# Hybrid S5, attention and mixture-of-experts block: gelu in two halves, each behind its own S5 outputs

## The chip, the cores and the metric

One core of a Trainium2 chip runs the whole block in one launch. The metric is the device time of an execution in microseconds, lower is better; a kernel's time is the median of several executions. TensorE (PE) does the matmuls, VectorE (DVE), ScalarE (ACT) and GpSimd (POOL) the elementwise work, and the queue of SyncE (SP) issues nearly all loads.

## The reference

The input is 256 tokens of 1024 channels. What the block computes, shortened:

```python
h = rms_norm(x, ln1_g)
u, q, k, v, gates = split(h @ w_in)                 # 512, 512, 512, 512, 2048 columns
y_ssm = s5_mixer(u, ...)                            # 32 groups, 64 complex states: a scan over the tokens
g = gelu(y_ssm)                                     # tanh form, 512 channels
y_ssm = g * sigmoid(g @ w_glu + b_glu)
y_attn = moba_attention(q, k, v, rel_bias)          # 8 heads; 256 tokens are one block, so causal softmax
merged = sigmoid(gate_ssm) * (y_ssm @ w_up_ssm) + sigmoid(gate_attn) * (y_attn @ w_up_attn)
x = x + merged @ w_out
x = x + hier_moe(rms_norm(x, ln2_g), ...)           # 32 experts, w1, w3: 1024 x 512, w2: 512 x 1024, two per token
return rms_norm(x, ln_f_g)
```

## The kernel before

The **front** is everything up to the router: the input projection as sixteen column slices (units `in0` to `in15`, 256 columns each, run in the order 0 to 8, 12, 9, 13, 10, 14, 11, 15), the GLU matmul (unit `glu`, which runs between `in11` and `in15`), the up projections (`up0` to `up3`) and the output projection (`out0` to `out3`). Units from `in12` on, `glu`, `up` and `out` run in split precision: a weight slice is loaded (`raw`, two buffers, blocks 2 and 3), cast to a high part `wh`, the difference goes to a low part `wl` (`split`, lines 711 and 714, two buffers of each), and three products are summed on PE. While a unit's matmuls run, the next unit's slice is split and the one two units on is loaded (`next_raw`).

The **back** is the mixture of experts: 8 quads of 4 experts, every quad 24 pieces of 1 MB of weights (16 of w1 and w3, 8 of w2), so 192 pieces in all. `pump` issues one piece each on the SP queue into the next of 22 slots (`KN['slots']`); a slot is one of the kernel's blocks of 1 MB, and most blocks hold something else in the front. A piece whose block is still in use waits at the head of the SP queue. `KN['after']` says how many pieces are issued behind the load of which unit: 15 in the front, the other 7 of the first 22 behind `out3`.

**Background threads** (`pool_thread`, `ssm_thread`, `attn_thread`, `gelu_thread`) are generators. `bg()` runs one step of those that are due after each quarter of an input slice's matmuls; the table `KN['g']` gives how many ticks a step waits, `KN['e']` which engine does an elementwise operation (V is DVE, A is ACT, G is POOL; E is "expand directly on the engine that multiplies"). So the tables set the order in which instructions stand in each engine's queue, and each engine runs its queue in that order. What is left of the threads when `glu` is reached is emitted in one go (`while threads: bg()`), ahead of the GLU matmuls.

The S5 part works on four channel groups j of 128 channels, in two halves hb (groups 0 and 1, then 2 and 3): prepare `W1e` and `Pe`, transpose into `M1s`, matmul `stp` (`s5_S`), scan on DVE, matmul `yp` (`s5_y`), then `s5_out` (lines 1149 and 1151) writes the outputs `yT`. Block 10 (`Uy`) holds the S5 inputs `U` and the outputs `yT`. Attention runs in two halves of four heads; its result `ya` sits in block 15, the block that the second half's scan coefficients `E` held. `gelu_thread` waits for the whole of S5 and of attention, and writes `gel` to block 8 and its split `gHL` to block 11; per group it is ACT square (`q`), DVE (`a`), ACT tanh (`t`), DVE (`b`), then the split (`s`).

Of the kernel before, what the change touches and what calls it, by code (L numbers as in the profile page):

```python
# [50 lines left out]
for _n, _w in (("ident", 128), ("tri", 128), ("iota1", 32), ("iota0", 32), ("rev", 32)):  # L51
# [391 lines left out]
       'geluge0a': 0,  # L443
       'geluge0b': 30,
       'geluge0q': 1,
       'geluge0s': 22,
       'geluge0t': 0,
       'geluge1a': 0,
# [1 line left out]
       'geluge1q': 1,  # L450
       'geluge1s': 6,
       'geluge1t': 26,
       'geluge2a': 26,
       'geluge2b': 13,
       'geluge2q': 1,
       'geluge2s': 16,
       'geluge2t': 1,
       'geluge3a': 40,
       'geluge3b': 5,
       'geluge3q': 1,  # L460
       'geluge3s': 22,
       'geluge3t': 13,
# [118 lines left out]
    'pump': {'glu0.0': 1,  # L581
       'glu0.1': 0,
       'in10.0': 0,
       'in10.1': 1,
       'in11.0': 0,
       'in11.1': 1,
       'in12.0': 0,
       'in12.1': 0,
       'in13.0': 0,
       'in13.1': 0,  # L590
       'in14.0': 0,
       'in14.1': 1,
       'in15.0': 1,
       'in15.1': 0,
       'in7.1': 0,
       'in8.1': 0,
       'in9.0': 0,
       'in9.1': 0,
       'out0.0': 0,
       'out0.1': 2,  # L600
       'out1.0': 0,
       'out1.1': 0,
       'out2.0': 0,
       'out2.1': 20,
       'up0.0': 2,
       'up0.1': 0,
       'up1.0': 1,
       'up1.1': 0,
       'up2.0': 0,
       'up2.1': 0,  # L610
       'up3.0': 1,
       'up3.1': 0},
    'slots': [16, 18, 20, 19, 21, 10, 11, 22, 8, 15, 17, 14, 13, 9, 12, 3, 2, 4, 0, 1, 6],
# [35 lines left out]
KN['pump'] = {}
KN['after'] = {'in9': 1, 'in11': 2, 'glu': 2, 'in15': 1, 'up1': 2, 'up3': 2, 'out0': 1, 'out1': 2, 'out2': 1}  # L650
KN['nw'] = 1
KN['warm'] = 10
KN['SL'] = 1
KN['after'] = {'in9': 1, 'in11': 2, 'glu': 2, 'in15': 1, 'up1': 2, 'up3': 2, 'out0': 1, 'out1': 2, 'out2': 1}
KN['slots'] = [20, 16, 18, 17, 21, 19, 10, 11, 8, 22, 13, 15, 12, 14, 9, 3, 7, 2, 4, 0, 1, 6]
# [1454 lines left out]
```

## Time and profile before

| | us |
|---|---|
| three runs | 662.68, 664.0, 664.91 |
| median | 664.0 |
| the profiled execution, its own time | 664.66 |
| its span, from the first to the last instruction | 662.9 |

The profiled execution is 0.66 us above the median. All rows further down are of it, and their clock starts at the span's first instruction. A mean clock of TensorE of 0.859 stands for a mix of its two levels, 1.2 and 2.4 GHz (0.50 and 1.00).

### The profile page before, as it was taken

How to read it: one execution, taken by the hardware profiler on the slowest of the kernel's cores; microseconds unless marked ns; L12 is line 12 of the kernel's file. 1: busy time of each engine (PE TensorE's matmuls, PEld its weight loads, DVE VectorE, ACT ScalarE, POOL GpSimd, SP SyncE). 2: the span in 40 equal slices, each digit the busy share in tenths (PEclk: the TensorE clock that was granted, in tenths of full speed). 3: DMA queues.
4: the chain of work that ended last, by engine and by line, in shares of the span. 5: the costliest groups of instructions: out<-in, count | busy, mean ns of one | idle time of the engine just before them, and what ended most of it. 6: DMA issues, size and time to landing. Idle time of an engine off the chain costs nothing.

```text
span 662.9 us, 9490 instructions
## 1 busy us (share of the span) xinstructions
PE 526.3 (79%) x3903; PEld 287.1 (43%) x3903; DVE 204.6 (31%) x403; ACT 122.8 (19%) x280; POOL 137.6 (21%) x235
## 2 busy tenths in 40 slices
PE   8989999979999789886786667767767767686772
PEld 7768799969987435340042014102300410140121
DVE  5854998867684331110020011001101000111012
ACT  3461644665213010000010000001000000000111
POOL 4896855735453000000000000000000000000012
PEclk9999998998999699897669679766976886787877
DMA  8527353976897899999999999999999999999992
GB/s 304 190 75 242 130 223 128 360 276 224 304 375 294 337 421 426 426 426 426 427 427 426 428 427 426 426 428 426 427 427 426 428 427 426 427 426 425 428 405 85
DMA packets 35152, 235.00 MB, mean 355 GB/s; under 512 B 4051, under 2 KB 5244, under 8 KB 7452
## 3 DMA queue, kind: packets, MB, share of 16 engines
q1 hardware_dynamic: 34412, 231.98, 85.6%
q0 software_dynamic: 256, 1.74, 1.0%
q8 instruction: 32, 0.52, 0.3%
q10 hardware_dynamic: 432, 0.59, 0.3%
q14 instruction: 20, 0.16, 0.1%
HBM read 233.23 MB, written 2.63 MB: 356 GB/s over the span
## 4 chain that ended last, share of the span: by engine, by line
DMA 63%; PE 14%; DVE 8%; POOL 8%; ACT 3%; issue 3%; SPq 0%; ACTq 0%; POOLq 0%; DVEq 0%
DMA wslot<-in_w 56%; PE inp L1304 3%; PE pa L1899 2%; PE pb L1899 2%; DVE wl L714 1%; PE xgp L1880 1%; DMA rbz<-rbd 1%; PE py L1956 1%; PE glp L1478 1%; DMA raw<-in_w_up 1%; DMA raw<-in_w_out 1%; DMA xc<-in_x_ch 1%; DMA rbd<-t 1%; DMA raw<-in_w_in 1%; DVE mt L714 1%
## 5 line engine op out<-in xcount | busy, mean ns | idle before, releaser
L1899 PE MATMUL pb<-wslot,xg 128*32 128x512 f32 x512 | 91.5, 797 | 37.0 <-DMA wslot<-in_w 36.9
L1899 PE MATMUL pa<-wslot,xg 128*32 128x512 f32 x512 | 89.7, 782 | 34.4 <-DMA wslot<-in_w 34.4
L1956 PE MATMUL py<-wslot,mt 128*32 128x256 f32 x1024 | 73.0, 431 | 20.3 <-DMA wslot<-in_w 14.8
L1858 POOL DMA_DIRECT2D lnf<-in_ln_f x1 | 0.6, 607 | 386.2 <-DMA wslot<-in_w 386.2
L1942 DVE SCALAR_TENSOR_TENSOR mt<-mt,pa 128x512 f32<-128x512 f32 x8 | 5.5, 688 | 240.0 <-ACT mt L1941 240.0
L1899 PEld LDWEIGHTS pb<-wslot,xg 128*32 128x32 f32 x512 | 13.4, 123 | 109.7 <-DMA wslot<-in_w 95.2
L1956 PEld LDWEIGHTS py<-wslot,mt 128*32 128x32 f32 x1024 | 32.3, 121 | 61.2 <-DMA wslot<-in_w 27.1
L1899 PEld LDWEIGHTS pa<-wslot,xg 128*32 128x32 f32 x512 | 12.2, 121 | 99.2 <-DMA wslot<-in_w 86.5
L714 POOL TENSOR_TENSOR wl<-raw,wh 128x512 fp32r<-128x512 f32 (+1 forms) x22 | 39.4, 1795 | 29.8 <-ACT wh L711 22.3
L1882 DVE TENSOR_TENSOR xg<-xgp,sm 128x512 f32<-128x512 f32 (+2 forms) x19 | 11.5, 608 | 80.8 <-PE xgp L1880 80.8
L1971 PE MATMUL xacc<-mt 128*128 128x512 f32 x56 | 30.2, 666 | 5.3 <-ACT mt L1968 5.3
L1880 PEld LDWEIGHTS xgp<-mt,x 128*128 128x128 f32 x256 | 30.9, 200 | 6.9 <-issue 6.1
L1880 PE MATMUL xgp<-mt,x 128*128 128x128 f32 x256 | 32.8, 287 | 1.1 <-DVE mt L1873 1.1
L1941 ACT ACTIVATE mt<-pa 128x512 f32<-128x512 f32 x8 | 4.8, 597 | 155.1 <-PE pa L1899 155.1
L1968 ACT COPY mt<-py 128x512 f32<-128x512 f32 (+1 forms) x17 | 9.5, 561 | 120.9 <-PE py L1956 120.9
L714 DVE TENSOR_TENSOR wl<-raw,wh 128x512 fp32r<-128x512 f32 (+1 forms) x26 | 28.7, 1112 | 9.9 <-ACT wh L711 7.7
L1300 PE MATMUL inp<-hn,raw 128*128 128x256 f32 x128 | 28.7, 380 | 1.1 <-DVE vu L1319 1.1
L1304 PE MATMUL inp<-hH,wh 128*128 128x256 f32 x112 | 29.2, 296 | 0.0
L1304 PE MATMUL inp<-hL,wh 128*128 128x256 f32 x112 | 28.5, 289 | 0.0
L1300 PEld LDWEIGHTS inp<-hn,raw 128*128 128x128 f32 x128 | 23.9, 190 | 4.9 <-DVE vu L1319 1.8
L711 ACT CAST wh<-raw 128x512 fp32r<-128x512 f32 (+1 forms) x28 | 20.6, 768 | 20.2 <-POOL wl L714 9.2
L1304 PEld LDWEIGHTS inp<-hH,wh 128*128 128x128 f32 x112 | 22.2, 198 | 0.3 <-issue 0.2
(322 smaller groups left out, 734.9 us busy)
## 6 DMA issues: line engine op xcount, KB each, us to landing
wslot<-in_w SPq DMA_DIRECT2D x191, 1024.0 KB, 19.6
raw<-in_w_in SPq DMA_DIRECT2D x14, 1024.0 KB, 5.1
raw<-in_w_up SPq DMA_DIRECT2D x4, 1024.0 KB, 7.2
raw<-in_w_out SPq DMA_DIRECT2D x4, 1024.0 KB, 6.8
rbz<-rbd POOLq DMA_DIRECT2D x1, 1536.0 KB, 8.4
xc<-in_x_ch SPq DMA_DIRECT2D x4, 256.0 KB, 5.1
raw<-in_w_in SPq DMA_DIRECT2D x4, 256.0 KB, 5.9
raw<-in_w_in SPq DMA_DIRECT2D x2, 512.0 KB, 7.4
```

Source lines behind the costliest of these rows:

```text
L711: (A.copy if e is A else e.tensor_copy)(out_, in_)
L714: pick_engine(name, default, opts).tensor_tensor(out=out, in0=in0, in1=in1, op=op)
L1300: T.matmul(ps[:, 0:S], raws["in", u][:, k, c], (h32 if u < 3 else hn)[:, k], start=(k == 0), stop=(k == KD - 1))
L1304: T.matmul(ps[:, 0:S], (wh if x else wl)[:, k, c], (hH if y else hL)[:, k], start=first, stop=last)
L1478: T.matmul(ps[:, 0:S], (glh if x else gll)[:, k, c], (gH if y else gL)[:, k], start=first, stop=last)
L1880: T.matmul(ps[:, i * 128:i * 128 + 128], h2[:, b, k * 128:k * 128 + 128], Dts[:, b].rearrange("p e s -> p (e s)"), start=(b == 0), stop=(b ...
L1882: V.tensor_tensor(out=xg[:, ks[0]:ks[0] + n], in0=ps[:, 0:n * 128].rearrange("p (k n) -> p k n", k=n), in1=smc("g2", ks[0], ks[0] + n).uns ...
L1899: T.matmul(pab[t][32 * e:32 * e + 32], xg[:, k, 32 * e:32 * e + 32], w[:, e], start=(k == 0), stop=(k == KD - 1))
L1942: V.scalar_tensor_tensor(out=hid, in0=hid, scalar=1.0, in1=pab[0], op0=OP.add, op1=OP.mult)
L1956: T.matmul(py[32 * e:32 * e + 32, n % 2 * 256:n % 2 * 256 + 256], hidT[:, f, 32 * e:32 * e + 32], w[:, i, e], start=(f == 0), stop=(f == 3))
L1968: A.copy(ye[:, o % 512:o % 512 + m], py[:, o % 512:o % 512 + m])
L1971: T.matmul(xacc[2 * b + o // 512], DwT[:, b], ye, start=(qd == 0), stop=(qd == NQ_RUN - 2))
```

## The change

`gelu_thread` no longer waits for all of S5 and all of attention: it runs on groups 0 and 1 as soon as their outputs are written, and on groups 2 and 3 behind theirs. Its result overwrites the S5 inputs `U` of the same groups, which have no reader left by then. The split `gHL` goes to block 8, once the last scores of attention have read q and k there. The attention result `ya` goes to block 20 (the first half's `E`), no longer to block 15. Steps of the two groups alternate: q, q, a, a, t, t, b, b, split, split. The tables of engines, ticks and flush positions are new throughout; about 30 elementwise operations change engine. The slots and the places of the 15 early pieces are laid out anew: the piece behind `in9` and one of the two behind `glu` move to `up0` and `up2`.

```diff
-       'W3.0': 'V',
+       'W3.0': 'G',
...
-       'glu.1l': 'V',
+       'glu.1l': 'G',
...
-       'P1.1.1': 'V',
+       'P1.1.1': 'G',
...
-KN['slots'] = [20, 16, 18, 17, 21, 19, 9, 10, 11, 8, 22, 13, 15, 12, 14, 3, 7, 2, 4, 0, 1, 6]
-KN['after'] = {'in9': 1, 'in11': 2, 'glu': 2, 'in15': 1, 'up0': 1, 'up1': 2, 'up3': 2, 'out0': 1, 'out1': 2, 'out2': 1}
+    'slots': [16, 18, 17, 15, 21, 19, 11, 8, 10, 22, 9, 13, 20, 12, 14, 3, 7, 2, 4, 0, 1, 6],
+    'after': {'glu': 1, 'in11': 2, 'in15': 1, 'out0': 1, 'out1': 2, 'out2': 1, 'up0': 2, 'up1': 2, 'up2': 1, 'up3': 2},
...
             s5_out(j1, y1)
+            st["done"].add(("yo", j1))
             yield "yo%d" % j1
...
-                yield from until("scan", 1)
+                yield from until("scan", 0)
...
-                    yaH, yaL = carve(blk(15, "ya", F32R), (4, S), (4, S))
+                    yaH, yaL = carve(blk(20, "ya", F32R), (4, S), (4, S))
...
     def gelu_thread():
-        yield from until("ssm")
-        yield from until("attn")
-        gel, ge1 = carve(blk(8, "gel"), (4, S), (4, S))
-        if "glu" in native:
-            gH = gL = None
-        else:
-            gH, gL = carve(blk(11, "gHL", F32R), (4, S), (4, S))
-        st["g"] = gel, gH, gL
-
-        for j in range(4):
-            n = "ge%d" % j
-            A.activation(out=ge1[:, j], in_=yT[:, j], func=AF.Square, scale=math.sqrt(0.044715))
-            yield n + "q"
-            V.scalar_tensor_tensor(out=ge1[:, j], in0=ge1[:, j], scalar=1.0, in1=yT[:, j], op0=OP.add, op1=OP.mult)
-            yield n + "a"
-            A.activation(out=ge1[:, j], in_=ge1[:, j], func=AF.Tanh, scale=math.sqrt(2.0 / math.pi))
-            yield n + "t"
-        for j in range(4):
-            n = "ge%d" % j
-            V.scalar_tensor_tensor(out=gel[:, j], in0=ge1[:, j], scalar=1.0, in1=yT[:, j], op0=OP.add, op1=OP.mult)
-            yield n + "b"
-            if "glu" not in native:
-                split(n + "s", gel[:, j], gH[:, j], gL[:, j])
-                yield n + "s"
+        gel = [U[:, 4 * j:4 * j + 4].rearrange("p q c -> p (q c)") for j in range(4)]
+        st["g"] = [gel, None, None]
+
+        for js in ((0, 1), (2, 3)):
+            yield from until("yo", js[-1])
+            for f, n in enumerate("qatb"):
+                for j in js:
+                    if f == 0:
+                        A.activation(out=gel[j], in_=yT[:, j], func=AF.Square, scale=math.sqrt(0.044715))
+                    elif f == 2:
+                        A.activation(out=gel[j], in_=gel[j], func=AF.Tanh, scale=math.sqrt(2.0 / math.pi))
+                    else:
+                        V.scalar_tensor_tensor(out=gel[j], in0=gel[j], scalar=1.0, in1=yT[:, j], op0=OP.add, op1=OP.mult)
+                    yield "ge%d%s" % (j, n)
+            if "glu" in native:
+                continue
+            if js[0] == 0:
+                yield from until("scores")
+                st["g"][1:] = carve(blk(8, "gHL", F32R), (4, S), (4, S))
+            for j in js:
+                split("ge%ds" % j, gel[j], st["g"][1][:, j], st["g"][2][:, j])
+                yield "ge%ds" % j
```

Line numbers of the changed kernel are 31 to 34 lower than those of before in this part: 1445 and 1451 (DVE) become 1413, 1443 is 1409, 1447 is 1411, 1388 is 1357, 711 and 714 are 677 and 680.

**DVE, from the last softmax of attention to the end of gelu**, before (`yp` are the S5 outputs in PSUM, `pv` the attention outputs, `wl<-raw,wh` the split of the GLU weights):

```order
L1385 TENSOR_SCALAR fs<-fs 128x4
L1149 STREAM_TRANSPOSE Uy<-yp 128x2x4x32
L1151 SCALAR_TENSOR_TENSOR Uy<-vu,sm,Uy 128x256
L1149 STREAM_TRANSPOSE Uy<-yp 128x2x4x32
L1151 SCALAR_TENSOR_TENSOR Uy<-vu,sm,Uy 128x256
L714 TENSOR_TENSOR wl<-raw,wh 128x4x256 x2
L714 TENSOR_TENSOR ya<-pv,ya 128x256 x2
L1445 SCALAR_TENSOR_TENSOR gel<-gel,Uy 128x256 x4
L1451 SCALAR_TENSOR_TENSOR gel<-gel,Uy 128x256
L711 CAST gHL<-gel 128x256
L1451 SCALAR_TENSOR_TENSOR gel<-gel,Uy 128x256 x3
L714 TENSOR_TENSOR gHL<-gel,gHL 128x256
```

The same place in the changed kernel:

```order
L1354 TENSOR_SCALAR fs<-fs 128x4
L680 TENSOR_TENSOR wl<-raw,wh 128x4x256
L1115 STREAM_TRANSPOSE Uy<-yp 128x2x4x32
L1117 SCALAR_TENSOR_TENSOR Uy<-vu,sm,Uy 128x256
L1115 STREAM_TRANSPOSE Uy<-yp 128x2x4x32
L1117 SCALAR_TENSOR_TENSOR Uy<-vu,sm,Uy 128x256
L1413 SCALAR_TENSOR_TENSOR Uy<-Uy 128x256 x4
L680 TENSOR_TENSOR gHL<-Uy,gHL 128x256
L680 TENSOR_TENSOR ya<-pv,ya 128x256 x2
```

Gelu of groups 2 and 3 now stands ahead of the attention result, one split of the GLU weights ahead of the S5 outputs, the other on POOL; groups 0 and 1 are gone from here.

**ACT, from the cast of `in9` (before) to the casts of `in9` and `in13`** (`M1s<-m1p` copies the transposes that `stp` needs, `Pe` and `s5a` are S5 coefficients), before:

```order
L711 CAST wh<-raw 128x8x128
L1044 COPY Pe<-s5a 64x8x16
L1045 ACTIVATE Pe<-s5a 64x8x16
L1332 ACTIVATE thg<-inp,fs 128x256
L1044 COPY Pe<-s5a 64x8x16
L1045 ACTIVATE Pe<-s5a 64x8x16
L711 COPY attB<-ptp 128x512
L711 COPY Pe<-pprep 64x4x4x16 x2
L1332 ACTIVATE thg<-inp,fs 128x256
L711 COPY Pe<-pprep 64x4x4x16 x2
L711 COPY M1s<-m1p 128x512
L711 CAST wh<-raw 128x8x128 x2
```

The same place in the changed kernel, to the first cast, which is that of the second half of `in9`:

```order
L1357 ACTIVATE attB<-attB,fs 128x128 x4
L1409 ACTIVATE Uy<-Uy 128x256 x2
L1010 COPY Pe<-s5a 64x8x16
L1011 ACTIVATE Pe<-s5a 64x8x16
L677 COPY Pe<-pprep 64x4x4x16 x2
L1411 ACTIVATE Uy<-Uy 128x256
L1299 ACTIVATE thg<-inp,fs 128x256
L1411 ACTIVATE Uy<-Uy 128x256
L677 COPY attB<-ptp 128x512
L1299 ACTIVATE thg<-inp,fs 128x256
L677 CAST wh<-raw 128x8x128
L677 COPY M1s<-m1p 128x512
```

(The pair of lines 1010 and 1011 stands there twice.) Squares and tanh of groups 0 and 1 have come in, and four scalings of the softmax that DVE did; the cast of the first half of `in9` (now on DVE) and two `Pe` copies have gone, and the copy to `M1s` stands behind the first cast.

**The SP queue, from the loads of `in12`, `in9`, ... to `up0`**, before:

```order
L795 DMA wslot<-in_w 128x2048
L1354 DMA attA<-rbz 128x4x256
L761 DMA raw<-in_w_in 128x2048 x4
L795 DMA wslot<-in_w 128x2048 x2
L761 DMA raw<-in_w_glu 128x2048
L795 DMA wslot<-in_w 128x2048 x2
L761 DMA raw<-in_w_in 128x2048
L795 DMA wslot<-in_w 128x2048
L761 DMA raw<-in_w_up 128x2048
L795 DMA wslot<-in_w 128x2048
```

The same place in the changed kernel:

```order
L1321 DMA attA<-rbz 128x4x256
L727 DMA raw<-in_w_in 128x2048 x4
L761 DMA wslot<-in_w 128x2048 x2
L727 DMA raw<-in_w_glu 128x2048
L761 DMA wslot<-in_w 128x2048
L727 DMA raw<-in_w_in 128x2048
L761 DMA wslot<-in_w 128x2048
L727 DMA raw<-in_w_up 128x2048
L761 DMA wslot<-in_w 128x2048 x2
```

By the load of `up0`, 6 pieces have been issued in place of 7 (the row behind it included); behind `up2` both have issued 9, and 15 ahead of `out3`.

## Rows read from the trace of the kernel before

**Rows 1.** The page, 40 slices of the span (tenths of a slice): DMA busy.

```profile
DMA  8527353976897899999999999999999999999992
```

**Rows 2.** The page, chain that ended last, by line.

```profile
DMA wslot<-in_w 56%; PE inp L1304 3%; PE pa L1899 2%; PE pb L1899 2%; DVE wl L714 1%; PE xgp L1880 1%; DMA rbz<-rbd 1%; PE py L1956 1%; PE glp L1478 1%; DMA raw<-in_w_up 1%; DMA raw<-in_w_out 1%; DMA xc<-in_x_ch 1%; DMA rbd<-t 1%; DMA raw<-in_w_in 1%; DVE mt L714 1%
```

**Rows 3.** Table by stage: stretch, length; busy PE, PEld, DVE, ACT, POOL; clock; DMA; GB/s.

```profile
157.40:187.00 29.60, 29.18 (x243) 28.98 (x242) 22.30 (x32) 10.64 (x24) 15.65 (x12) 1.00 0.89 342
187.00:212.00 25.00, 24.17 (x106) 18.18 (x106) 16.96 (x24) 6.30 (x15) 11.73 (x10) 1.00 0.84 318
241.00:640.00 399.00, 294.87 (x2190) 94.34 (x2186) 31.49 (x55) 21.54 (x39) 0.61 (x1) 0.80 1.01 426
```

**Rows 4.** SP queue in order of time: start, us, instruction, count (two windows).

```profile
203.46 9.90 SPq L795 DMA_DIRECT2D wslot<-in_w  x7
...
224.55 2.03 SPq L795 DMA_DIRECT2D wslot<-in_w  x2
```

**Rows 5.** Chain in order of time, 144 to 170 us: start, us, what.

```profile
144.31 2.57 issue
...
150.02 7.50 PE glp L1478 x43
157.52 5.15 PE inp L1304 x43
...
162.73 7.23 DMA raw<-in_w_up
```

**Rows 6.** PE in order of time; in brackets idle time and what ended it.

```profile
109.53 1.80 PE L1103 MATMUL stp<-Uy,M1s 128*128 128x64 f32 x11 [1.51 <-ACT M1s L711]
...
146.89 0.36 PE L1478 MATMUL glp<-gHL,wh 128*128 128x256 f32 x1 [2.60 <-DVE gHL L711]
```

**Rows 7.** Table by stage, two stretches of low clock; columns as in rows 3.

```profile
110.00:113.80 3.80, 3.80 (x22) 3.80 (x22) 3.70 (x8) 0.78 (x1) 0.00 (x0) 0.56 0.60 246
...
148.00:154.80 6.80, 6.26 (x26) 5.57 (x26) 5.08 (x8) 3.84 (x7) 3.85 (x7) 0.50 0.14 46
```

**Rows 8.** DVE in order of time, 138 to 150 us.

```profile
138.64 0.48 DVE L1151 SCALAR_TENSOR_TENSOR Uy<-vu,sm,Uy 128x256 f32<-128x256 f32 x1
139.04 2.35 DVE L714 TENSOR_TENSOR wl<-raw,wh 128x1024 fp32r<-128x1024 f32 x2
...
143.22 0.43 DVE L1445 SCALAR_TENSOR_TENSOR gel<-gel,Uy 128x256 f32<-128x256 f32 x1 [0.79 <-ACT gel L1443]
...
148.95 0.42 DVE L714 TENSOR_TENSOR gHL<-gel,gHL 128x256 fp32r<-128x256 f32 x1 [0.47 <-ACT gHL L711]
```

**Rows 9.** ACT in order of time, 136 to 149 us.

```profile
136.89 1.27 ACT L1388 ACTIVATE attB<-attB,fs 128x128 f32<-128x128 f32 x4 [1.30 <-DVE fs L1385]
...
141.54 0.42 ACT L1443 ACTIVATE gel<-Uy 128x256 f32<-128x256 f32 x1
...
147.98 0.94 ACT L711 CAST gHL<-gel 128x256 fp32r<-128x256 f32 x2 [1.45 <-DVE gel L1451]
```

**Rows 10.** ACT in order of time, 93 to 111 us.

```profile
93.05 1.05 ACT L711 CAST wh<-raw 128x1024 fp32r<-128x1024 f32 x1 [4.03 <-DMA raw<-in_w_in]
...
97.22 0.81 ACT L711 COPY Pe<-pprep 64x256 f32<-64x256 f32 x2
98.66 1.99 ACT L711 CAST wh<-raw 128x1024 fp32r<-128x1024 f32 x2
...
107.58 1.04 ACT L711 CAST wh<-raw 128x1024 fp32r<-128x1024 f32 x1 [3.36 <-DMA raw<-in_w_in]
...
108.90 0.58 ACT L711 COPY M1s<-m1p 128x512 f32<-128x512 f32 x1
```

**Rows 11.** DVE, 98 to 105 us, and POOL, 99 to 105 us, in order of time.

```profile
98.47 0.85 DVE L1016 TENSOR_TENSOR Pe<-pprep 64x256 f32<-64x256 f32 x2
...
100.13 5.04 DVE L1016 TENSOR_TENSOR Pe<-pprep 64x256 f32<-64x256 f32 x2
...
99.78 5.11 POOL L714 TENSOR_TENSOR wl<-raw,wh 128x1024 fp32r<-128x1024 f32 x2 [6.66 <-ACT wh L711]
```

More of the change, by code (lines that the diff above doesn't have):

```diff
@@ L127 @@
        'U2.1': 'A',
-       'U2.2': 'G',
+       'U2.2': 'V',
        'U2.3': 'A',
@@ L161 @@
        'Wx1.1': 'E',
-       'Wx2.0': 'E',
-       'Wx2.1': 'E',
+       'Wx2.0': 'A',
+       'Wx2.1': 'A',
        'Wx3.0': 'E',
@@ L203 @@
        'gz2h': 'A',
-       'gz2l': 'G',
+       'gz2l': 'V',
        'gz3h': 'V',
@@ L214 @@
        'hb3': 'G',
+       'ke5.1': 'V',
        'm1l': 'V',
+       'm25': 'V',
+       'm5l': 'G',
        'm6h': 'V',
-       'nm0.128': 'V',
+       'nm0.128': 'A',
        'nm0.256': 'V',
@@ L268 @@
        'up0.0.0l': 'G',
-       'up0.0.1h': 'V',
+       'up0.0.1h': 'A',
        'up0.0.1l': 'V',
@@ L282 @@
        'up1.1.1l': 'V',
-       'up2.0.0h': 'A',
+       'up2.0.0h': 'V',
        'up2.0.0l': 'G',
@@ L374 @@
        'in1.1': 1,
-       'in10.0': 1,
-       'in10.1': 2,
+       'in10.0': 3,
+       'in10.1': 1,
        'in11.0': 1,
-       'in11.1': 1,
-       'in12.0': 1,
+       'in11.1': 2,
+       'in12.0': 3,
        'in12.1': 1,
@@ L393 @@
        'in5.0': 0,
-       'in5.1': 3,
+       'in5.1': 2,
        'in6.0': 1,
@@ L406 @@
        'attnex1.256': 3,
-       'attnmx0.128': 6,
-       'attnmx0.256': 4,
+       'attnmx0.128': 8,
+       'attnmx0.256': 5,
        'attnmx1.128': 0,
@@ L428 @@
        'attntc0.1': 1,
-       'attntc0.2': 21,
+       'attntc0.2': 18,
        'attntc1.0': 0,
        'attntc1.1': 0,
-       'attntc1.2': 1,
+       'attntc1.2': 3,
        'attntp0.0': 0,
@@ L442 @@
        'attnya1.1': 0,
[L443 to L448, printed above, removed]
-       'geluge1b': 3,
[L450 to L462, printed above, removed]
+       'geluge0a': 1,
+       'geluge0b': 1,
+       'geluge0q': 0,
+       'geluge0s': 1,
+       'geluge0t': 1,
+       'geluge1a': 1,
+       'geluge1b': 3,
+       'geluge1q': 0,
+       'geluge1s': 1,
+       'geluge1t': 1,
+       'geluge2a': 0,
+       'geluge2b': 0,
+       'geluge2q': 0,
+       'geluge2s': 0,
+       'geluge2t': 0,
+       'geluge3a': 1,
+       'geluge3b': 1,
+       'geluge3q': 0,
+       'geluge3s': 1,
+       'geluge3t': 1,
        'poolE0': 1,
        'poolE1': 4,
-       'poolP0.0': 1,
-       'poolP0.0.0': 1,
+       'poolP0.0': 0,
+       'poolP0.0.0': 3,
        'poolP0.0.1': 1,
@@ L552 @@
        'ssmsb1': 4,
-       'ssmsb2': 1,
+       'ssmsb2': 0,
        'ssmsb3': 0,
@@ L580 @@
     'glu': 15,
[L581 to L613, printed above, removed]
+    'pump': {'out2.1': 1},
+    'slots': [16, 18, 17, 15, 21, 19, 11, 8, 10, 22, 9, 13, 20, 12, 14, 3, 7, 2, 4, 0, 1, 6],
     'sp': {'in1.0': 3,
@@ L619 @@
        'in11.1': 2,
-       'in12.0': 0,
+       'in12.0': 2,
        'in12.1': 3,
@@ L632 @@
        'in4.0': 3,
-       'in4.1': 0,
+       'in4.1': 3,
        'in5.0': 3,
@@ L647 @@
     'order': [0, 1, 2, 3, 4, 5, 6, 7, 8, 12, 9, 13, 10, 14, 11, 15],
-}
[L649 to L655, printed above, removed]
-KN['slots'] = [20, 16, 18, 17, 21, 19, 9, 10, 11, 8, 22, 13, 15, 12, 14, 3, 7, 2, 4, 0, 1, 6]
-KN['after'] = {'in9': 1, 'in11': 2, 'glu': 2, 'in15': 1, 'up0': 1, 'up1': 2, 'up3': 2, 'out0': 1, 'out1': 2, 'out2': 1}
+    'after': {'glu': 1, 'in11': 2, 'in15': 1, 'out0': 1, 'out1': 2, 'out2': 1, 'up0': 2, 'up1': 2, 'up2': 1, 'up3': 2},
+    'nw': 1,
+    'warm': 10,
+    'SL': 1,
+}
 OPTS = {}
@@ L1473, in glu_mm @@
             for k in range(4):
-                T.matmul(ps[:, 0:S], raws["glu"][:, k, c], gel[:, k], start=(k == 0), stop=(k == 3))
+                T.matmul(ps[:, 0:S], raws["glu"][:, k, c], gel[k], start=(k == 0), stop=(k == 3))
             return
@@ L1485, in glu_evac @@
         if "up" in native:
-            V.scalar_tensor_tensor(out=ysH[:, b], in0=z, scalar=1.0, in1=gel[:, b], op0=OP.add, op1=OP.mult)
+            V.scalar_tensor_tensor(out=ysH[:, b], in0=z, scalar=1.0, in1=gel[b], op0=OP.add, op1=OP.mult)
         else:
-            V.scalar_tensor_tensor(out=z, in0=z, scalar=1.0, in1=gel[:, b], op0=OP.add, op1=OP.mult)
+            V.scalar_tensor_tensor(out=z, in0=z, scalar=1.0, in1=gel[b], op0=OP.add, op1=OP.mult)
             split("gz%d" % b, z, ysH[:, b], ysL[:, b])
```

34 lines of the change are left out of this document (18 added, 16 removed).

## The prediction

> **What bounds the kernel now.** I read the chain of waits first. More than half of it is the loads of expert weights [rows 2], so the question is how long that stream lasts and when it starts. The slices of the page show the DMA engines full from the 15th slice of 40 to the end [rows 1]. The table by stage says the same with numbers: from 241 to 640 us the DMA share is 1.01 at 426 GB/s, while PE is busy 294.87 of 399 us [rows 3]. A piece of 1.049 MB then takes 1.049/0.426 = 2.46 us. Nothing the engines do in that stretch changes the end; the number of pieces still to come does.
>
> Next, the SP queue where the front meets the back. The last 7 of the first 22 pieces are issued from 203.46 to 213.36 us. The next is issued at 224.55, when the first expert matmuls give back a slot [rows 4]. So all 22 slots have been filled by then, and 170 pieces remain: 170 x 2.46 = 418 us, to 643, with a tail behind it up to 662.9. The start of the back therefore carries the end one to one: a front that is 1 us shorter is a kernel that is 1 us shorter, as long as the 22 slots still fill in time.
>
> So I read the front for what sets its end. From 157.4 to 212 us PE is busy 29.18 + 24.17 = 53.35 of 54.6 us, at full clock [rows 3]: it is fed nearly without a break. What PE loses before 157 is not made good behind it. The chain in order of time shows the largest loss: the last `in11` matmul ends at 144.31, and the first `in15` matmul starts at 157.52 [rows 5]. Between them lie the 48 GLU matmuls (4 output blocks of 12 products). `in15` does 43 such matmuls in 5.15 us, 0.12 each [rows 5], so 48 need 5.75. The stretch takes 13.21, so **7.46 us are lost**: first idle time until the split of gelu arrives [rows 6], then half clock, since from 148.0 to 154.8 the granted clock is 0.50 [rows 7], the lower of its two levels, which costs 6.8/2 = 3.4.
>
> **The change, part by part.**
>
> *Gelu of groups 0 and 1 leaves the stretch.* Its work is as before, some 4 us spread over ACT, DVE and POOL, now behind the first half's S5 outputs at about 92 us. What it does there is in the third part below.
>
> *Gelu of groups 2 and 3.* The S5 outputs end on DVE at 138.64 + 0.48 = 139.12 [rows 8], 5.2 us before PE runs out of `in11` matmuls. Gelu came only behind the attention result, and its four groups ended at 148.95 + 0.42 = 149.37 [rows 8]. Now one split of the GLU weights, 2.35/2 = 1.18, stands ahead of the S5 outputs, so they end at 140.3. From there the last group needs a square 0.42 (ACT) [rows 9], 0.43 (DVE), a tanh (taken at the square's 0.42), 0.43 again, the two casts 0.94 [rows 9] and a subtraction 0.42 [rows 8]: 3.06, with some 0.3 for six hand-overs 143.7. Group 2 runs in its shadow. PE reaches GLU at 144.31 with the same matmuls ahead of it (the S5 and attention matmuls only change places among those of `in11`). So the cover is `in11` itself, with 0.6 us to spare. It is thin, and one thing eats it: `glu.1l` has moved to POOL and runs there while DVE finishes the S5 outputs. The rows show what that can do: a pair of DVE expansions took 0.85 us with POOL idle and 5.04 beside two POOL subtractions of 5.11 together [rows 11], so a DVE instruction can lose up to one POOL subtraction, 2.5 us. Remaining wait of PE: between 0 and 2.5, and I take 1.3, the middle, since only the two-input instructions there overlap the POOL subtraction.
> The Trainium skill, SBUF — State Buffer, section "Who interferes with whom", makes this a rule: a VectorE instruction with two SBUF inputs and a GpSimd instruction that reads SBUF block each other for a whole instruction, whoever came second waiting. By that rule, which rows 11 bear out, moving `glu.1l`, `P1.1.1` and `W3.0` from DVE to POOL speaks against the change: it frees DVE of less than the time they take.
>
> *The new order around 86 to 112 us.* In the kernel before PE stands 1.51 us ahead of the second half's `stp` at 109.53 [rows 6], followed by a stretch of clock 0.56 from 110.0 to 113.8 [rows 7], 3.8 x 0.44 = 1.7 us of work lost. It waits for the copy to `M1s` at 108.90, which stands on ACT behind a cast at 107.58 that waits for a load [rows 10]. That load needs the buffer that the POOL subtractions from 99.78 free [rows 11], and these wait for the ACT cast at 98.66 [rows 10]. So the ACT run from 93.05 to 98.66, 5.61 us, sets `stp`. In the changed order it gains four scalings 1.27 [rows 9], two squares and two tanh 4 x 0.42, and sheds a cast 1.05, two `Pe` copies 0.81 and the `M1s` copy 0.58 [rows 10], net +0.5. But it needn't start with the load at 93.05: ACT stood idle 4.03 ahead of it [rows 10], and now begins with work that waits for DVE only, which has lost the softmax scaling. So the cast moves by between +0.5 and +0.5 - 4.03 = -3.5. I take -2.0, the middle less a little, for the first tanh and its DVE partner wait for each other. The same shift reaches `stp`, GLU and, PE being fed, everything behind.
>
> *From 157 us on.* The same operations, some on other engines: DVE is busy 22.30 of 29.6 and 16.96 of 25, POOL 15.65 and 11.73 [rows 3], so single splits of 1 us that change sides find room. Of the loads, two pieces more fall behind `up0`'s: 26 of 1 MB in place of 24, 64 us, in the 70 us from 144 to 214. The load of `up2`, on the chain for 7.23 us [rows 5], has as many pieces ahead of it as before. I take 0 here, and plus or minus 1.5 for the range. *`ya` in block 20, the new slots:* the blocks of the pieces in the front are free before their turn (`U` with the last GLU evaluation, `gHL` with the last GLU matmul), cost 0; the cover is SP's own wait for the next raw buffer. If a piece did wait there, the raw load behind it would be late by as much.
>
> **Sum.** -7.46 + 1.3 - 2.0 = -8.2 against the profiled execution's own 664.66: 656.5. That execution lies 0.66 above the median, so **655.8** for the median.
>
> **The rivals.**
> 1. *The second gelu comes late after all* (the lock of rows 11 hits twice, or the idle time is long enough for half clock): 2.5 idle in place of 1.3, and 1.7 lost to the clock as after `stp`, gives 655.8 + 2.9 = 658.7. For it: POOL's `glu.1l` and its two casts lie exactly there. Against it: 0.6 us of cover, and only the last of 48 matmul groups need group 3.
> 2. *The loads take part of it back*: PE comes 8 us sooner to `up0`, the DMA is already busy 0.89 and 0.84 of that stretch [rows 3], and the two moved pieces, 4.9 us, end up ahead of a raw load on the chain: 660.7. Against it: the stretch that vanishes is one in which the loads had little to do, so the load on the rest is nearly as before.
> 3. *Slower.* Gelu of groups 0 and 1 sits in ACT's queue ahead of the cast of `in9`. Each microsecond in which its squares and tanh wait for DVE passes through cast, POOL subtraction, load and `M1s` copy to `stp` at 109.53. The GLU stretch gives 6.2, so it decides once `stp` comes later than 115.7. Three DVE instructions there, each held up by one POOL subtraction of 2.5, make 7.5 in place of -2.0: -7.46 + 1.3 + 7.5 = +1.3, 665.3; four make 667.8. POOL has more to do there than before (`W3.0`, `P1.1.1`), which speaks for it; that ACT starts up to 4 us sooner speaks against.
> 4. *No difference*: rival 3 at half its price and rival 1 together, 655.8 + 2.9 + 4.5 = 663.2.
>
> **How the numbers follow.** This kernel's measurement can tell some 0.3%, 2 us, from no change. Chances: the forecast 0.53 (652.5 to 658), rival 1 0.20, rival 2 0.13, rival 4 0.07, rival 3 0.07. Rival 2 lies past the bound of 662.0 only at its far end (0.01 of its share). That makes faster 0.85, same 0.08, slower 0.07. The low end takes -7.46, no wait at GLU and -3.5, with the half clock behind `stp` kept: 653.0, less 1 for a better stretch from 157 on: 652.0. The high end is rival 2's 660.7 with a little more, 661.0; what lies above is rivals 3 and 4, 0.14.
>
> **What would show it.** Right: PE starts GLU within 1.5 us of the last `in11` matmul and the clock stays 1.00 there; GLU to `in15` takes 6 to 7.5 us in place of 13.21; `stp` of the second half starts at 106 to 109; the first slot comes back at about 216 in place of 224.55, and the DMA share behind it is 1.01 as before. Wrong: an idle PE ahead of GLU put down to `gHL` on POOL or DVE (rival 1), of an `up` or `out` matmul put down to a split behind a raw load (rival 2), or an `stp` later than 109.53 (rival 3).

## The result, and the profile after

The changed kernel takes **657.16 us** (median of 4 runs, 655.15 to 658.41) where the kernel before, run beside it, takes 664.41 (4 runs, 662.68 to 664.91): a ratio of 0.9893, 95% interval 0.9861 to 0.9924. The profiled execution took 657.07 us with a span of 655.3, 7.6 less than before. Forecast were 655.8 for the median and 656.5 for the profiled one.

The SP queue of the changed kernel in order of time, at the first slot given back, and below it the table by stage (columns as in [rows 3]):

```profile
216.58 8.52 SPq L761 DMA_DIRECT2D wslot<-in_w  x6
```

```profile
157.40:187.00 29.60, 27.80 (x196) 25.58 (x195) 23.67 (x37) 6.69 (x14) 16.05 (x14) 1.00 0.96 382
...
241.00:640.00 399.00, 285.95 (x2152) 90.51 (x2151) 30.70 (x53) 22.14 (x42) 3.15 (x3) 0.83 1.01 424
```

The first slot comes back at 216.58 in place of 224.55 [rows 4], 7.97 us earlier, and the span is 7.6 shorter. Behind it the DMA is as full as before, 1.01 [rows 3]. What is new stands in the first row: from 157.4 to 187 us the DMA share has risen from 0.89 to 0.96, and PE, busy 29.18 of 29.6 us before, now is busy 27.80.

PE of the changed kernel, its GLU, up and out matmuls by tile (calls, shortest/median/longest ns, start of the first and of the last):

```profile
L1445 PE MATMUL glp<-gHL,wh x32: 278/283/385, 141.7 to 147.3; 128*128 128x256 f32 x32
L1650 PE MATMUL upp<-ya,wh x64: 283/283/284, 153.7 to 177.1; 128*128 128x256 f32 x64
L1675 PE MATMUL acc<-wh,mH x32: 387/389/499, 179.2 to 202.8; 128*128 128x512 f32 x32
```

The same engine in order of time (the ends of idle times in brackets):

```profile
102.89 0.55 PE L1043 MATMUL m1p<-co,W1e 128*128 128x128 f32 x3 [2.76 <-ACT W1e L677]
...
106.59 0.67 PE L1069 MATMUL stp<-Uy,M1s 128*128 128x64 f32 x5
...
135.94 0.66 PE L1366 MATMUL ptp<-co,attB 128*128 128x128 f32 x4 [1.86 <-ACT attB L677]
...
147.90 0.28 PE L1271 MATMUL inp<-hH,wh 128*128 128x256 f32 x1
```

The last `in11` matmul ends at 141.88, GLU starts with no wait, and `in15` follows at 147.90: 6.0 us where the kernel before takes 13.1 (144.29 to 157.36). The median GLU matmul takes 283 ns, and the clock is 1.00 from 5.9 to 210.7 us. Two long waits are new, 2.76 us at 102.89 and 1.86 at 135.94, where `attB` holds the softmax of attention's second half. The up stretch, from the first `upp` to the first `acc` matmul, has become longer: 25.5 us, against 23.7 before (163.1 to 186.8). PE in order of time, its waits there in the changed kernel:

```profile
167.29 1.22 PE L1650 MATMUL upp<-ys,wh 128*128 128x256 f32 x8 [0.52 <-DVE wh L677]
168.77 0.50 PE L1650 MATMUL upp<-ys,wl 128*128 128x256 f32 x2 [0.26 <-POOL wl L680]
170.19 0.50 PE L1650 MATMUL upp<-ys,wl 128*128 128x256 f32 x2 [0.91 <-POOL wl L680]
```

Together PE waits 1.69 us for the split of a weight slice; the kernel before has one such wait, 0.42 us at 177.86. The chain leads back from these splits over DVE's queue to the load of `up2`, 7.63 us from 154.80. This is the sign that the prediction gave for its rival 2.

One gain lies where nothing was forecast, ahead of 82 us. `Wx0.0` is the expansion that makes a part of `W1e`, an S5 coefficient: before, DVE subtracts into a work buffer (`pprep`) and ACT copies that to `W1e`; now DVE writes `W1e` itself. Rows of before in order of time, of ACT, DVE, PE and SP:

```profile
33.20 5.26 ACT L711 COPY Uy<-vu 32x256 f32<-32x256 f32 x8
...
39.64 0.71 ACT L711 COPY W1e<-pprep 64x192 f32<-64x192 f32 x2
...
40.38 0.67 DVE L1065 TENSOR_TENSOR pprep<-s5a,fs 128x192 f32<-128x192 f32 x1 [6.31 <-ACT W1e L711]
...
43.77 0.55 PE L1077 MATMUL m1p<-co,W1e 128*128 128x128 f32 x3 [3.03 <-ACT W1e L711]
...
87.99 0.33 SPq L761 DMA_DIRECT2D raw<-in_w_in  x1
```

The copies stand on ACT behind eight copies of `Uy`, and DVE waits 6.31 us to reuse the work buffer. PE then waits 3.03 for the next part of `W1e`. The same places in the changed kernel:

```profile
33.23 0.84 DVE L982 TENSOR_TENSOR W1e<-pprep 64x192 f32<-64x192 f32 x2
...
34.44 0.52 DVE L1031 TENSOR_TENSOR pprep<-s5a,fs 128x192 f32<-128x192 f32 x1
...
82.23 0.33 SPq L727 DMA_DIRECT2D raw<-in_w_in  x1
```

DVE goes on at 34.44, PE's longest wait for `W1e` in this part is 0.71 us, and the raw load issued at 87.99 before goes out at 82.23. The changed kernel is 5.8 us ahead there, 2.4 at the end of `in11`, 9.5 at `in15`, 7.7 at `out` and 8.0 at the first slot.

### The profile page after: what moved, and what is told of

It is laid out like the page before. It is cut to its first block, busy times and chain, and to the rows that moved or that the text cites. A ratio compares the mean times of both kernels' runs of the same rounds, so it can differ in the third digit from the quotient of the medians.

```text
span 655.3 us, 9477 instructions
## 1 busy us (share of the span) xinstructions
PE 514.2 (78%) x3903; PEld 281.1 (43%) x3903; DVE 205.5 (31%) x398; ACT 123.1 (19%) x284; POOL 144.2 (22%) x239
## 4 chain that ended last, share of the span: by engine, by line
DMA 68%; DVE 15%; POOL 6%; PE 5%; issue 3%; ACT 2%; SPq 0%; POOLq 0%; ACTq 0%; DVEq 0%
DMA wslot<-in_w 62%; DVE wl L680 3%; DMA raw<-in_w_out 2%; DMA rbz<-rbd 1%; DMA raw<-in_w_up 1%; DVE wh L677 1%; DVE scan L1087 1%; DMA xc<-in_x_ch 1%; PE scp L1941 1%; PE py L1923 1%; PE xgp L1847 1%; DVE Pe L982 1%; DVE scan L680 1%; POOL E L970 1%; DMA attA<-rbz 1%
## 5 line engine op out<-in xcount | busy, mean ns | idle before, releaser
L1923 PE MATMUL py<-wslot,mt 128*32 128x256 f32 x1024 | 66.8, 399 | 28.1 <-DMA wslot<-in_w 22.5
L1923 PEld LDWEIGHTS py<-wslot,mt 128*32 128x32 f32 x1024 | 30.0, 113 | 65.2 <-DMA wslot<-in_w 34.0
L680 POOL TENSOR_TENSOR wl<-raw,wh 128x512 fp32r<-128x512 f32 (+1 forms) x23 | 41.8, 1821 | 26.4 <-DVE wh L677 15.4
L1938 PE MATMUL xacc<-mt 128*128 128x512 f32 x56 | 27.1, 606 | 5.3 <-ACT mt L1935 5.3
```

Of the source, the lines that this page charges most:

```text
L680: pick_engine(name, default, opts).tensor_tensor(out=out, in0=in0, in1=in1, op=op)
L1923: T.matmul(py[32 * e:32 * e + 32, n % 2 * 256:n % 2 * 256 + 256], hidT[:, f, 32 * e:32 * e + 32], w[:, i, e], start=(f == 0), stop=(f == 3))
L1938: T.matmul(xacc[2 * b + o // 512], DwT[:, b], ye, start=(qd == 0), stop=(qd == NQ_RUN - 2))
```

## The experiments

Theory 1 ahead of them was that of the prediction: PE feeds the front, and the GLU stretch gives the gain. All kernels ran beside the kernel before; the ratio is to it. GLU is the time from the end of the last `in11` matmul to the first of `in15`, up from the first `upp` to the first `acc` matmul, "load" how long after the first `upp` matmul the load of `up2` lands (before: 162.73 + 7.23 [rows 5], 6.8 us after 163.1), slot the time of the first slot given back. These four are of one execution of each kernel, the times are medians; executions of one kernel spread by 1.3 us (pieces_w9) to 8 us (before, 660.72 to 668.73 over all its runs).

| kernel | us, median (runs) | ratio, 95% | GLU | up | load | slot |
|---|---|---|---|---|---|---|
| before | 664.41 (4) | | 13.1 | 23.7 | 6.8 | 224.55 |
| changed | 657.16 (4) | 0.9893 [0.9861, 0.9924] | 6.0 | 25.5 | 8.8 | 216.58 |
| gelu_late | 659.94 (5) | 0.9928 [0.9902, 0.9954] | 12.4 | 23.1 | 5.9 | 221.41 |
| half0_late | 657.35 (11) | 0.9906 [0.9878, 0.9934] | 9.7 | 23.0 | 6.2 | 218.70 |
| old_tables | 664.60 (10) | 0.9996 [0.9978, 1.0014] | 5.6 | 30.3 | 10.9 | 226.56 |
| old_pieces | 660.66 (6) | 0.9936 [0.9911, 0.9961] | 5.6 | 24.3 | 7.4 | 222.26 |
| pieces_late | 659.92 (10) | 0.9937 [0.9915, 0.9959] | 6.0 | 29.3 | 10.8 | 222.46 |
| pieces_early | 654.17 (6) | 0.9844 [0.9821, 0.9868] | 6.0 | 23.0 | 6.0 | 214.99 |
| wx00_act | 661.62 (12) | 0.9961 [0.9942, 0.9980] | 5.6 | 23.2 | 6.5 | 221.04 |
| before_wx00 | 662.20 (12) | 0.9951 [0.9926, 0.9975] | 13.1 | 23.8 | 6.9 | 223.30 |
| p110_pool | 659.55 (6) | 0.9919 [0.9889, 0.9949] | 6.0 | 24.9 | 8.1 | 219.93 |
| pieces_px110 | 654.24 (5) | 0.9844 [0.9820, 0.9869] | 6.0 | 23.0 | 6.0 | 213.72 |
| pieces_w9 | 654.48 (6) | 0.9858 [0.9824, 0.9891] | 6.1 | 23.0 | 5.8 | 214.66 |
| glu1l_dve | 656.71 (5) | 0.9892 [0.9869, 0.9914] | 5.6 | 25.8 | 9.0 | 216.16 |

The columns up and load go together in all rows. Up takes 23.0 to 23.2 us where the load of `up2` lands up to 6.5 us behind up's start; from there each microsecond later is one more of up (6.9: 23.8, 8.1: 24.9, 9.0: 25.8), and near 11 us, where half clock comes on top, up takes 29 to 30. pieces_late, pieces_early and old_pieces below move the loads alone.

**gelu_late**: the place of gelu alone undone.

```diff
+        yield from until("ssm")
+        yield from until("attn")
         for js in ((0, 1), (2, 3)):
-            yield from until("yo", js[-1])
```

> Only the place of gelu is undone: both halves wait for the S5 outputs and for the attention result, as in the kernel before; the tables, slots and loads are those of the changed kernel. Theory 1 (the gain is the GLU stretch, 13.21 us before and 6.2 after): the stretch is 12 to 13.5 us again, the first slot comes back at 222 to 225 us and the kernel takes 662 to 665. Rival (the gain is the new order of the first 82 us, where PE was 5.8 us ahead): the first slot stays at 216 to 218 and the kernel takes 656 to 659.

PE of gelu_late in order of time, in GLU:

```profile
143.62 0.35 PE L1446 MATMUL glp<-gHL,wh 128*128 128x256 f32 x1 [1.17 <-DVE gHL L677]
...
146.26 0.58 PE L1446 MATMUL glp<-gHL,wh 128*128 128x256 f32 x1 [0.67 <-ACT gHL L677]
```

The table by stage, a stretch of GLU:

```profile
146.00:152.80 6.80, 6.31 (x28) 6.02 (x29) 5.47 (x10) 3.82 (x7) 2.62 (x5) 0.50 0.18 65
```

The waits and the half clock (0.50) in GLU are back, and GLU takes 12.4 us, as theory 1 said. But the kernel does not fall back: the slot comes at 221.41, 4.8 later than with the change and not 8, and the ratio moves from 0.9893 to 0.9928, 0.35% or 2.3 us, with intervals that overlap. Neither theory held. By the times the place of gelu is worth about a third of the gain, by the slot more than half; the two intervals allow anything from nothing to 5 us. While PE stands in GLU the DMA share is 0.18, and the up stretch behind takes 23.1 us in place of 25.5. The wait of 2.76 us at 102.89 falls to 1.00 here, and to 1.01 in half0_late, the two runs in which gelu's first half is not done ahead of it; by the end of `in11` this is given back (142.45 here, against 141.88).

**half0_late**: only the first half of gelu moved back, behind the last S5 output.

```diff
-            yield from until("yo", js[-1])
+            yield from until("yo", 3)
```

> In the changed kernel only the first half of gelu is moved: it waits for the last S5 output too, as the second half does, and neither waits for the attention result. Theory 1 (each half's place is worth part of the GLU stretch): all four groups fall behind 139.7, PE waits 1 to 2.5 us ahead of or in GLU, which takes 7.5 to 9.5 us in place of 6.2; the up stretch takes part of it back, so the first slot comes back at 217.3 to 219 in place of 216.58 and the kernel takes 657.5 to 660. Rival (only the wait for the attention result mattered, the engines do four groups as soon as two): GLU within 0.7 us of 6.2 and 656 to 658.

GLU takes 9.7 us, a little over theory 1's range: three waits of 0.36 to 0.68 us and a stretch of half clock. `in15` starts 3.7 us later; up gives 2.5 back, the slot comes 2.1 later, in theory 1's range, and the time, in the rival's, can't be told from that of the changed kernel.

**old_tables**: the new code, slots and places of pieces, with the tables of before (24 entries of engines, 10 of the order, 5 of fillers and 3 of copies go back; the 19 order entries of gelu stay).

```diff
-       'Wx0.0': 'E',
+       'Wx0.0': 'A',
...
-       'glu.1l': 'G',
+       'glu.1l': 'V',
...
```

> The code, the slots and the places of the loads are those of the changed kernel; the tables that lay out engines, the background order, the fillers and the split copies are those of the kernel before, but for gelu's own entries in the order. Theory 1 (the gain is the GLU stretch; what the new order gives before 82 us is given back before GLU): the GLU stretch takes 6 to 8.5 us, the first slot comes back at 216 to 219, 656 to 660 us in all. Rival (the new order carries the gain): the first slot at 222 to 226, 662 to 666.

PE of old_tables, its GLU, up and out matmuls by tile:

```profile
L1995 PE MATMUL glp<-gHL,wh x32: 283/283/283, 146.1 to 151.3; 128*128 128x256 f32 x32
L2200 PE MATMUL upp<-ya,wh x64: 278/283/416, 157.6 to 185.9; 128*128 128x256 f32 x64
L2225 PE MATMUL acc<-wh,mH x20: 387/389/496, 187.9 to 201.7; 128*128 128x512 f32 x20
```

PE in order of time, its longest wait in up:

```profile
173.47 1.22 PE L2200 MATMUL upp<-ys,wh 128*128 128x256 f32 x8 [1.78 <-DVE wh L1227]
```

The chain in order of time, from a load of the up stage to the cast that this wait ends with:

```profile
159.47 9.02 DMA raw<-in_w_up
...
168.59 1.15 ACT wh L1227 x2
...
169.82 1.31 DVE wl L1230
...
173.08 0.35 DVE wh L1227
```

The table by stage, the stretch behind the wait:

```profile
175.40:182.20 6.80, 5.89 (x28) 5.84 (x28) 5.76 (x8) 1.87 (x5) 5.63 (x5) 0.50 0.86 311
```

GLU takes 5.6 us with no wait at all, and the kernel gains nothing: the rival's time, with the slot at 226.56, later than either theory gave. This refutes theory 1 as it stood. `in11` ends 2.0 us later than in the kernel before, and `upp` to `acc` takes 30.3 us: PE waits 1.78 us for a cast on DVE. The chain leads back from that cast over DVE's queue and a split to the load of `up2`, which takes 9.02 us. The half clock behind the wait costs 6.8/2 = 3.4 more.

**old_pieces**: old_tables with the expert pieces ahead of the up stretch, as in pieces_early (below).

> The tables of before as in old_tables, with the earlier pieces of pieces_early. Theory 1 (with the old tables the GLU stretch gives its 7 us too, and the up stretch loses 6.6 because raw loads go out behind expert pieces): the up stretch falls from 30.3 us to 24 to 26.5, the first slot comes back at 221 to 223.5, 659 to 662 us. Rival (the load of up0 itself is late, at 147.87, since its buffer waits for a split of the GLU weights that stands behind gelu): the up stretch stays at 28 to 30.5 and the kernel at 663 to 665.5.

Up falls from 30.3 to 24.3 us, the slot to 222.26 and the kernel to 660.66: theory 1 of this run on every number. The load of `up0` still goes out at 147.61; that it is late is not what costs. So with the old tables the new code (gelu's place, with the new blocks and slots) is worth some 4 us once the up loads don't queue behind pieces, less at most 0.7 that earlier pieces could give the kernel before (up 23.7 in place of 23.0).

**pieces_late** and **pieces_early**: the changed kernel, the places of the pieces alone.

```diff
-    'after': {'glu': 1, 'in11': 2, 'in15': 1, 'out0': 1, 'out1': 2, 'out2': 1, 'up0': 2, 'up1': 2, 'up2': 1, 'up3': 2},
# pieces_late
+    'after': {'in11': 2, 'in15': 0, 'glu': 0, 'out0': 1, 'out1': 2, 'out2': 1, 'up0': 3, 'up1': 3, 'up2': 1, 'up3': 2},
# pieces_early
+    'after': {'in11': 2, 'glu': 2, 'in15': 2, 'up0': 1, 'up1': 1, 'up2': 1, 'up3': 2, 'out0': 1, 'out1': 2, 'out2': 1},
```

> The opposite of pieces_early: in the changed kernel two expert pieces more go out behind the loads of up0 and up1, and two fewer behind those of glu and in15. Theory 1 (a piece ahead of a raw load of the up stretch costs PE up to its 2.46 us): the up stretch takes 27.5 to 30.5 us in place of 25.5, the first slot comes back at 218.5 to 221.5 and the kernel takes 659 to 663. Rival (the splits on DVE and POOL set the up stretch): it stays within 0.8 us of 25.5 and the kernel at 656 to 658.5.

> Only the places of the expert pieces among the other loads are changed in the changed kernel: four of those that lie behind the loads of the up stage go out from in11 to in15, where the DMA was partly idle. Theory 1 (the 1.5 us that the up stretch lost are raw loads that wait behind pieces): out starts 1 to 1.5 us earlier, at 177.7 to 178.2 in place of 179.16, and the kernel takes 655 to 656.5. Rival (the loss is in the splits on DVE and POOL, or the pieces only collide with the raw loads earlier): 656.5 to 659.

The load of `up2` by tile (issue; us to landing), of the changed kernel, then of pieces_early with its up stretch:

```profile
L727 SPq DMA_DIRECT2D raw<-in_w_up x1: 328/328/328, 154.8 to 154.8; - x1
DMA to landing us min/median/max: 7.6/7.6/7.6
```

```profile
L728 SPq DMA_DIRECT2D raw<-in_w_up x1: 328/328/328, 154.8 to 154.8; - x1
DMA to landing us min/median/max: 4.9/4.9/4.9
...
L1651 PE MATMUL upp<-ya,wh x64: 283/283/283, 153.7 to 174.7; 128*128 128x256 f32 x64
L1676 PE MATMUL acc<-wh,mH x32: 387/390/502, 176.8 to 201.2; 128*128 128x512 f32 x32
```

Issued at the same time, the load lands 2.7 us sooner with fewer pieces ahead. Two pieces more behind the loads of the up stage make up 29.3 us; pieces_early, with two fewer there (not four, as its expectation says), makes it 23.0 with no wait left: theory 1 in both. In pieces_late the slot comes 1 us later than it gave, in pieces_early `out` starts 0.9 earlier and the time lies 0.8 below its range. With 654.17 us, 0.9844, pieces_early is 1.6% faster than the kernel before and 0.5% faster than the changed one; these last two intervals just overlap.

**wx00_act** and **before_wx00**: the one entry of ahead of 82 us, undone in the changed kernel, and made in the kernel before.

```diff
# wx00_act
+KN['e']['Wx0.0'] = 'A'
# before_wx00
+KN['e']['Wx0.0'] = 'E'
```

> One entry changed in the changed kernel: the expansion Wx0.0 is again copied by ACT, as in the kernel before, in place of being written by DVE itself. Theory 1 (this entry is why PE no longer waits 3.03 us for W1e at 43.77, and what it gains passes to GLU): PE waits 2.5 to 3.1 us there again, the raw load of 82.23 goes out at 84.7 to 86, the last in11 matmul ends at 143.5 to 145 in place of 141.88, and the kernel takes 659 to 661.5. Rival (it is given back at the waits before GLU, or other entries do it): the last in11 matmul within 1 us of 141.88 and 656 to 658.5.

PE and SP of wx00_act in order of time:

```profile
43.62 0.55 PE L1044 MATMUL m1p<-co,W1e 128*128 128x128 f32 x3 [2.97 <-ACT W1e L678]
...
86.96 0.33 SPq L728 DMA_DIRECT2D raw<-in_w_in  x1
```

The wait at 43.6 is back, the raw load 4.7 us later, the end of `in11` at 147.21 and the kernel at 661.62, 0.68% or 4.5 us slower: theory 1, with more at the load and at `in11` than it gave and just above its time. The slot comes 4.5 us later, about as much as in gelu_late (4.8): this one entry is worth as much here as the place of gelu, by the times rather more.

> The kernel before with one entry changed: the expansion Wx0.0 is written by DVE itself, as in the changed kernel, in place of copies by ACT. Theory 1 (more than half of the gain is this entry and has nothing to do with gelu): the wait of 3.03 us at 43.77 falls below 1, the raw load of 87.99 goes out at 82.5 to 85, the first slot comes back at 219.5 to 222 in place of 224.55 and the kernel takes 659 to 662. Rival (the entry only works with the rest of the new order, or the waits ahead of GLU swallow it): the raw load after 86 or the first slot after 223, 662.5 to 665.

Made alone in the kernel before, the entry takes the wait away, and the raw load goes out at 84.40 in place of 87.99, but only 2.2 us of that reach `in15` (155.16) and 1.25 the slot (223.30, the rival's); 662.20 lies between the two theories. By the ratio it is worth 3.3 us. Of the 5.8 us ahead of 82 the entry thus gives 3.6 alone and 4.7 in the changed kernel; what gives the rest no run separates.

**p110_pool**, **pieces_px110** and **pieces_w9**: the wait at 102.89. There DVE's expansion `P1.1.0` runs beside two POOL subtractions. DVE, POOL and ACT of the changed kernel in order of time:

```profile
94.81 5.10 DVE L982 TENSOR_TENSOR Pe<-pprep 64x256 f32<-64x256 f32 x2
...
94.71 4.91 POOL L680 TENSOR_TENSOR wl<-raw,wh 128x1024 fp32r<-128x1024 f32 x2 [3.09 <-issue]
...
102.13 0.71 ACT L677 COPY W1e<-pprep 64x192 f32<-64x192 f32 x2 [5.75 <-DVE pprep L984]
```

```diff
# p110_pool: the changed kernel and
+KN['e']['P1.1.0'] = 'G'
# pieces_px110: pieces_early and
+KN['e']['Px1.1.0'] = 'A'
# pieces_w9: pieces_early and
+KN['e']['w9.1l'] = 'V'
```

> One entry changed in the changed kernel: the expansion P1.1.0 on POOL in place of DVE, which takes a DVE work of 5.10 us out from beside POOL's subtractions at 94.7. Theory 1 (this expansion and the subtractions hold each other up, and that is the 2.76 us for which PE waits at 102.89): that wait falls below 1 us, the last matmul of in11 ends at 139 to 140 in place of 141.88, and the kernel takes 654 to 656. Rival (the attention chain, which delays PE at 135.94, or POOL, which has more to do, sets the arrival at GLU): 656.5 to 659, with the time lost at another place before GLU.

> The changed kernel with the earlier pieces of pieces_early and one entry more: the expansion Px1.1.0 is copied by ACT, which stands idle there for 5.75 us, so that DVE makes one subtraction beside POOL's in place of two expansions. Theory 1 (the expansions and POOL's subtractions hold each other up, and the 2.76 us of PE at 102.89 are their price): that wait falls below 1 us, the last in11 matmul ends at 139.5 to 140.5, the first slot comes back at 212.5 to 213.5 in place of 214.99, and the kernel takes 651.5 to 653. Rival (a raw load or the attention chain sets the arrival at GLU): the first slot at 214.5 to 215.5 and 653.5 to 655.

> The changed kernel with the earlier pieces of pieces_early and one entry more: the subtraction w9.1l, the first of the two on POOL at 94.7, on DVE ahead of the expansion P1.1.0, so that only one POOL subtraction is left for DVE to meet. Theory 1 (each POOL subtraction can hold up one DVE instruction): DVE's part from 94.0 to 102.0 ends 1 to 2.5 us earlier, the wait of 2.76 us at 102.89 falls below 1.5, the raw load of 97.11 goes out 1 to 2.4 us earlier, the last in11 matmul ends at 139.5 to 141 and the kernel takes 651.5 to 653.5. Rival (the attention chain gives the time back ahead of GLU, as in pieces_px110): the last in11 matmul at 141.5 to 142.3 and 653.5 to 655.5.

In p110_pool the wait is gone, as theory 1 said, but POOL, with the expansion on top, is late with a split at 109.68 (PE waits 1.80), and `in11` ends at 143.84, 2 us later: the rival, with 0.5 us more. In pieces_px110 DVE has one subtraction there in place of two, and the next two-input instruction takes its place, as its DVE shows in order of time:

```profile
95.07 2.54 DVE L986 TENSOR_TENSOR pprep<-pprep 128x256 f32<-128x256 f32 x1
97.54 2.56 DVE L1033 TENSOR_TENSOR pprep<-s5a,fs 128x192 f32<-128x192 f32 x1
```

The wait is still 1.89 us, and `in11` ends at 141.82: the rival again by its time, though the slot, 213.72, comes 0.8 earlier than it gave. In pieces_w9, with one POOL subtraction left, the pair of expansions takes 3.26 us in place of 5.10, but DVE has the other subtraction to do itself and ends this part at 102.05, as before (102.09). The raw load goes out at 95.81 in place of 97.15, the wait stays 2.75, and `in11` ends at 141.41, 0.5 earlier than in pieces_early: the rival's time. None of the three is faster than the kernel that it was made from. In all three the wait for `attB` at 134 to 138 is what PE meets last ahead of GLU; what is won at 102.89 ends there.

**glu1l_dve**: one split of the GLU weights back on DVE.

```diff
+KN['e']['glu.1l'] = 'V'
```

> One entry changed in the changed kernel: the subtraction glu.1l on DVE, as in the kernel before, in place of POOL. Theory 1 (beside POOL's subtraction the DVE instructions lose what moving it saves, so POOL taking it relieves DVE of nothing): the second half's S5 outputs end within 0.6 us of 139.7, the last matmul of in11 and the first of GLU lie within 0.6 us of 141.8, and the kernel takes 655.5 to 659. Rival (DVE is relieved by it): the S5 outputs end over 1.2 us later, PE waits 1 us or more ahead of GLU or the load of up0 goes out later than 139.5, and the kernel takes 659 to 662.

DVE's first S5 output in order of time, in the changed kernel (POOL runs `glu.1l` from 135.09 for 3.25 us) and in glu1l_dve (POOL idle there):

```profile
136.68 1.94 DVE L1117 SCALAR_TENSOR_TENSOR Uy<-vu,sm,Uy 128x256 f32<-128x256 f32 x1
```

```profile
136.78 0.49 DVE L1118 SCALAR_TENSOR_TENSOR Uy<-vu,sm,Uy 128x256 f32<-128x256 f32 x1
```

With a split more to do, DVE ends its S5 outputs at 138.36, 1.35 us *earlier* than the 139.71 of the changed kernel; the split itself runs at 140.10, behind gelu's own work. The load of `up0` goes out 3 us later, at 141.35, which by the rival would have cost; the time is the same, 656.71. That is theory 1, and further than its number: POOL taking the split relieves DVE of nothing. The Trainium skill, SBUF — State Buffer, "Who interferes with whom", which the prediction weighed, states that a DVE instruction with two SBUF inputs contends with a GpSimd instruction that reads SBUF. The trace agrees: 1.94 us beside POOL's subtraction, 0.49 without it.

## Why the prediction was right, and where it was not

The time was right, but partly by luck: errors in it cancel, and the reason given most weight was not enough by itself. Ahead of 82 us the kernel won 5.8 us that were not forecast, and from there to the end of `in11` it did 5.4 worse than forecast; GLU gave 0.9 more than reckoned, and the up stretch took 1.8 that stood in no sum.

*The stream of expert weights sets the end, one to one with the first slot*: right to within some 2 us. From the first slot to the end of the span it is 436.1 to 439.9 us in all 14 kernels (438.35 before, 438.7 after). In gelu_late, at 436.1, 4.8 us of the slot are therefore 2.2 of the span; why it differs between executions is not shown.

*The GLU stretch, -7.46 + 1.3*: right in the stretch, which gave 7.1. (It took 13.1 us before, not 13.21: the first `in15` matmul starts at 157.36, ahead of the chain's 157.52.) The 48 matmuls take 5.6 us where nothing disturbs them (5.75 was reckoned), waits and their after-effects 0.4 in place of 1.3, and the clock stays at 1.00. A POOL subtraction did hold up one S5 output (1.94 us), as feared, and the cover held.

*What PE loses in the front carries to the end*: this is the step that failed. The prediction took PE as fed from 157 us on, and so each microsecond of GLU as one of the end. gelu_late shows 6.4 us of GLU as 4.8 of the slot; half0_late 3.7 of GLU as 2.1; in old_tables 7.5 come to nothing, with 6.6 lost in the up stretch and 2.0 ahead of GLU.

*From 157 us on, 0 plus or minus 1.5*: it was +1.8. Rival 2 named the mechanism, loads that take part back, and priced it at 4.9; its argument against itself, that the stretch that vanishes had little to load, was the mistake. That stretch is where the DMA caught up: its share was 0.14 there before [rows 7]. With the changed kernel's pieces it costs 1.8, with two pieces more (pieces_late) 5.6, with the old tables 6.6, with two fewer (pieces_early) nothing.

*The new order around 86 to 112 us, -2.0*: the sum was nearly right (`in11` ends 2.4 earlier), the cause wrong. The new order had won 5.8 us ahead of 82, where the prediction costed the new tables at nothing without reading that stretch's waits; and from 82 to 142 it lost 3.4 in place of winning 2.0. It is true that ACT begins with gelu's work, but it then stands idle 5.75 us for a DVE that the POOL subtractions hold up. What [rows 11] show, weighed in the sum only where gelu's second half lies, met DVE's work right behind gelu's first half. `stp` came at 106.59, within the 106 to 109 forecast, by luck.

*Rival 1* did not come about: PE starts GLU without a wait. *Rival 2* did in part, 1.8 us of its 4.9. *Rival 3*: two DVE instructions were held up by a POOL subtraction each, as it priced them, but PE lost 2.76 us by it (at 102.89), far from deciding.

Open is why `old_tables` and `wx00_act` reach `in11` as late as they do (146.26 and 147.21, against 144.29 before): the entry costs 4.7 us at 87 and 5.3 at `in11`, and no run separates the attention chain from the rest there.
